# Modulation chunks in float32 and in three bfloat16 parts on four column groups, with another start-up order

## The chip, the cores and the metric

One core of a Trainium2 chip runs the kernel. Its engines are TensorE (PE, with its weight loads as PEld), VectorE (DVE), ScalarE (ACT), GpSimd (POOL) and SyncE (SP, which here only issues DMAs). The metric is device microseconds for one launch, lower is better.

## The reference, cut to what matters

Two blocks in sequence. The first has two layers over 256 tokens `x` and 256 context tokens `ctx`, width 1024; the second has two hybrid layers over `x` alone. The part that the change touches is the modulation of the first block: two condition vectors, `c` and `c_ctx`, go through one wide matrix per layer, and the twelve results scale, shift and gate the streams.

```python
def adaln(cond, w_ada, b_ada):
    m = jax.nn.silu(cond) @ w_ada + b_ada          # w_ada: 1024 x 6144 for each layer
    return jnp.split(m, 6, axis=-1)
...
    for l in range(DEPTH):                          # DEPTH = 2
        h = rms_norm(x, g_mix[l]) * (1 + sc1) + sh1
        hc = rms_norm(ctx, g_mix[l]) * (1 + csc1) + csh1
        ... h @ w_in, attention, Fourier mix ...
        x = x + gt1 * (o @ w_out[l])
        x = x + gt2 * swiglu(rms_norm(x, g_ffn[l]) * (1 + sc2) + sh2, w_gate[l], w_up[l], w_down[l])
        # the same for ctx in layer 0 only
```

Everything is float32.

## The kernel before, in words

**Weights.** All weights come as raw float32 tiles of 128x2048 (1 MB) on SP's queue, through three buffers (`raw`). For each 128x1024 piece ScalarE makes a rounded copy `whi` (L210) and VectorE the remainder `wlo` (L211), five buffers each. Products are three passes (`mm3`, L330 to L332): high by high, and the two cross terms.

**The modulation.** The 1024x6144 matrix of a layer is cut into 12 chunks of 512 columns, two raw tiles each; `(l, c)` is chunk c of layer l. `ada_chunk` (L463) splits four pieces into `whi` and `wlo` and runs 16 matmuls, with the four columns of `s4` (high and low part of both condition vectors) as the stationary operand and 512 weight columns moving (L480, L481). ScalarE copies the 4x512 result (L483), four small transposes put it on the partitions (L485), and three VectorE operations (L491 to L494) add the parts and the bias into `mod`. Chunk (1, 11) alone is `whole`: eight float32 matmuls on the raw tile (L475), no split.

**Where the chunks lie.** Chunks 2, 0, 3, 1 of layer 0 come before the first projection: chunk 2 ahead of the norms (L757), the others from `ada_start`. Two lie in the middle of layer 0's attention (`ada_mid`), four around its output projection (`ada_att`), six in its feed-forward steps (`ada_ffn`, keyed by the step f//2 of eleven). Layer 1's attention has two in `ada_mid` and four in `ada_att`, and two stand behind its second norm (`ada_gap`, L822).

**Start-up.** SP issues the identity, the conditions, `vec`, chunk 2's two raw tiles, then the context and the residual (`cs`, `xs`, 1 MB each, L760). Squares are made by ScalarE (L763) and summed over the eight k-tiles by one VectorE reduction per stream (L764); `sum_cols` (L351) sums over partitions by matmuls against a column of ones, and a chain of small VectorE operations and a transpose (`rsqrt`, `spread` L363) gives the row scale. Then two halves of the contraction follow in turn: gain, the weights' half, `modulate` of both streams (L520 to L522), 48 matmuls into four banks.

**Order.** The order on each engine is fixed when the program is built, by a scheduler that takes ready instructions by priority, in program order unless a function is `ranked` or stands in `together`, which moves a run of matmuls far ahead and lets it start after the operations it names. In the feed-forward network each step takes four pieces of gate and up weights and 96 matmuls of 512 columns; after steps 3, 7 and 10 the down projection of the group follows in `dn` banks. The attention sums `pv` (L625) already put two heads on two groups of 64 columns of the array, one behind the other.

Of the kernel before, what the change touches and what calls it, by code (L numbers as in the profile page):

```python
# [18 lines left out]
P = 128  # L19
KT = 8  # L20
# [195 lines left out]
        self.off = off  # L216


class WRows(Weights):


# [34 lines left out]
class Build:  # L256
# [17 lines left out]
    ada_whole = ((1, 11),)  # L274

    rank = {"weights": 100, "weigh": -200, "qk": -200, "rope": -300, "hd2": -300, "together": 3000}

    def __init__(self, ctx, tc, d, out):
        self.tc, self.nc, self.d, self.out = tc, tc.nc, d, out
# [180 lines left out]
            h0 += n  # L460


    def ada_chunk(self, l, c):  # L463

        nc = self.nc
        ps = self.bank("mm")
        off = (l * 12 + c) * P * 4096
        whole = (l, c) in self.ada_whole
        n = 2 if whole else 4
        if whole:  # L470
            for i in range(2):
                raw = self.wp.tile([P, RAW], F32, tag="raw", name="raw", bufs=self.raw_bufs)
                nc.sync.dma_start(raw, self.d["w_ada"][off + i * P * RAW:off + (i + 1) * P * RAW].rearrange("(p f) -> p f", p=P))
                for k in range(4):
                    nc.tensor.matmul(ps[:2, :], self.sil[:, 4 * i + k, :], raw[:, 512 * k:512 * k + 512], start=i + k == 0, stop=i == 1 and k == 3)  # L475
        else:
            ch = WRows(self, self.d["w_ada"], off, 512)
            for k in range(KT):
                hi, lo = ch.get(k)
                nc.tensor.matmul(ps[:4, :], self.s4[:, k, :], hi, start=k == 0, stop=False)  # L480
                nc.tensor.matmul(ps[:4, :], self.s4[:, k, :], lo, start=False, stop=k == KT - 1)  # L481
        rows = self.b1.tile([4, 512], F32, tag="rows", name="rows", bufs=1)
        nc.scalar.copy(rows[:n], ps[:n, :])  # L483
# [4 lines left out]
        src = ps[:, :8].rearrange("p (a b) -> p a b", b=2)  # L488
        if not whole:
            m = self.sp.tile([P, 4, 2, 2], F32, tag="adac", name="adac", bufs=2)  # L490
            nc.vector.tensor_copy(m.rearrange("p a b c -> p (a b c)"), ps[:, :16])  # L491
            nc.vector.tensor_tensor(dst, m[:, :, :, 0], m[:, :, :, 1], op=ALU.add)
            src = dst
        nc.vector.tensor_tensor(dst, src, b[:, :, None].to_broadcast([P, 4, 2]), op=ALU.add)  # L494

    def gain(self, l, which, ks=range(KT)):

# [6 lines left out]
    def norm_row(self, s):  # L504

        rb = self.acc[:, s * 256:s * 256 + 256]
        v = self.mean_eps(self.sum_cols(rb, 2), 2, D, "ms")
        self.nc.scalar.copy(rb, self.spread(self.rsqrt(v, 2, "rn"), 2))
        return rb

# [121 lines left out]
    def mixer1(self, l, h, o, first):  # L632
# [27 lines left out]
        for kind in range(2):  # L660
            ch = WRows(self, d["w_in"], base + (1 + kind) * P * 4096, 512)
            q0, f0 = (128, 0) if kind else (0, 384)
            for s in range(2 if full else 1):
                raws = [self.evac_raw(self.proj_t(ch, h, (2 * s + i,))[0], 512) for i in range(2)]
                if not kind:
                    r = self.head_rms(raws, 6, 0)
                for i in range(2):
                    q = raws[i][:, q0:q0 + 384]
                    if not kind:
                        self.scale_heads(q, r[:, 6 * i:6 * i + 6], 6)  # L670
                    if s == 0:
                        c, sn = (self.rc[:, i], self.rs[:, i]) if kind else (self.tqc[:, i], self.tqs[:, i])
                        q = self.rope(q, c, sn, 6, "rq")
                    elif not kind:
                        self.gain_heads(q, self.gq, 6)
                    dst = self.ap.tile([P, 6, P], F32R, tag="qt", name="qt", bufs=5)
                    self.to_qt(q, 6, dst)
                    self.qt[kind, 2 * s + i] = dst
                self.fourier(raws, f0, o[3 + kind], s * 256)
            for a in self.ada_mid[l] if kind else ():  # L680
                self.ada_chunk(*a)
            for s in range(2 if full else 1):
                self.heads1(kind, s, o)

# [36 lines left out]
    def block1(self, ctx):  # L721
# [7 lines left out]
        sil = self.sil = self.b1.tile([P, KT, 2], F32, name="sil")  # L729
        nc.scalar.activation(sil, ct, AF.Silu)  # L730
        self.s4 = self.b1.tile([P, KT, 4], F32R, name="s4")
        v = self.s4.rearrange("p k (s a) -> p k s a", a=2)
        nc.vector.tensor_copy(v[:, :, :, 0], sil)
        nc.vector.tensor_tensor(v[:, :, :, 1], sil, v[:, :, :, 0].bitcast(F32), op=ALU.subtract)
# [3 lines left out]
        nc.gpsimd.dma_start(wm, d["wm"])  # L738
# [12 lines left out]
        self.phase(self.att_banks)  # L751
        norm = ExitStack()
        self.np = norm.enter_context(tc.tile_pool(name="norm0", bufs=1, reuse_waits="tile"))
        nc.sync.dma_start(self.vec, d["vec"])
        nc.gpsimd.tensor_tensor(self.g12, self.vec[:, 128:136], self.vec[:, 136:144], op=ALU.mult)
        self.nt_bufs = 8
        self.ada_chunk(0, 2)  # L757
        rbs = [None, None]
        for s in (1, 0):
            nc.sync.dma_start(self.xs[s].rearrange("p a b -> p (a b)"), d["xT"][:, s * 2048:(s + 1) * 2048])  # L760
        for s in (1, 0):
            sq = self.np.tile([P, KT, 256], F32, tag="sq0", name="sq0", bufs=2)
            nc.scalar.activation(sq, self.xs[s], AF.Square)  # L763
            nc.vector.reduce_sum(self.acc[:, s * 256:s * 256 + 256], sq.rearrange("p k t -> p t k"), axis=AX.X)  # L764
            rbs[s] = self.norm_row(s)
        for l in range(2):

            both = (0, 1) if l == 0 else (0,)
# [3 lines left out]
            if l == 0:  # L772

                ps = [self.bank(tag) for tag in self.half_tags]
                for i in range(2):
                    ks = range(4 * i, 4 * i + 4)
                    for a in self.ada_start[i]:
                        self.ada_chunk(0, a)
# [9 lines left out]
                nc.sync.dma_start(c1, d["c1"])  # L788
                self.load_norms(l)
# [12 lines left out]
            for a in self.ada_att[l]:  # L802
                if isinstance(a, int):
                    self.out_first(l, a, o)
                else:
                    self.ada_chunk(*a)
            self.phase(self.lin_banks)
            norm = ExitStack()
            self.np = norm.enter_context(tc.tile_pool(name=f"norm{l + 1}", bufs=1, reuse_waits="tile"))
            with tc.tile_pool(name=f"ffn{l}", bufs=1, reuse_waits="tile") as fp:  # L810
                h = self.parts(fp, "F")
                for st in apart:
# [9 lines left out]
                    for a in self.ada_gap[l]:  # L822
                        self.ada_chunk(*a)
                f0 = 0
                dn = l * FT * P * 1024
                for gi, g in enumerate(FF_GROUPS):
                    acts = []
                    for f in range(f0, f0 + g, 2):
                        for a in self.ada_ffn[l].get(f // 2, ()):
                            self.ada_chunk(*a)  # L830
# [413 lines left out]
```

## Time and profile before

| | us |
|---|---|
| median of three runs (1584.55 to 1586.06) | 1584.88 |
| the profiled execution | 1584.88 |
| its span on the core | 1583.1 |
| PE busy in the span | 1535.0 |
| DVE busy | 1111.7 |
| ACT busy | 885.8 |

The span is the time from the first to the last instruction that the profile shows; the rest of the execution lies around it. A busy PE is not PE at its peak, since matmuls overlap and their records include the time to drain: two 512-column matmuls that each last 0.39 us can start 0.23 us apart. So PE work is counted from start to start.

### The profile page before, as it was taken

To read this page: it belongs to the slowest core of one execution; us is meant where nothing else is said; L and a number is where in the kernel's file an instruction comes from. 1 tells how busy PE (TensorE), PEld (TensorE's weight loads), DVE (VectorE), ACT (ScalarE), POOL (GpSimd) and SP (SyncE) were. 2 spreads that over 40 slices of the span, in tenths; PEclk is the share of its full clock that TensorE was granted. 3 is DMA by queue.
4 is the path that set the end of the run, shared out by engine and by line. 5 is a ranking of instruction groups with operands and counts; after the bars stand their busy time and mean duration, and the time that the engine had idled before them with its cause. 6 is when DMAs were issued, how large, how long until landed. Compare 5 with 4: busy or idle time off the path is not lost.

```text
span 1583.1 us, 25393 instructions
## 1 busy us (share of the span) xinstructions
PE 1535.0 (97%) x9826; PEld 1307.4 (83%) x9826; DVE 1111.7 (70%) x2332; ACT 885.8 (56%) x1590; POOL 71.0 (4%) x83
## 2 busy tenths in 40 slices
PE   4999999999999999999999999999999999999997
PEld 1776679878788778965779999998999999899997
DVE  7876988453433445989885555998867779987775
ACT  5567875342322234569764444667764456776542
POOL 0310000000000000010000000102000000201000
PEclk8999999999999999999999999999999999999998
DMA  7512443342332424444575554534344544334451
GB/s 285 199 54 81 173 160 136 132 164 104 133 107 81 149 98 162 154 156 156 201 261 181 184 179 161 170 139 152 115 160 160 184 142 155 133 117 170 146 178 51
DMA packets 36984, 238.38 MB, mean 151 GB/s; under 512 B 4224, under 2 KB 5888, under 8 KB 15104
## 3 DMA queue, kind: packets, MB, share of 16 engines
q1 hardware_dynamic: 36576, 236.14, 42.8%
q8 instruction: 77, 1.26, 0.3%
q0 software_dynamic: 288, 0.62, 0.3%
q14 instruction: 43, 0.35, 0.1%
HBM read 236.32 MB, written 1.05 MB: 150 GB/s over the span
## 4 chain that ended last, share of the span: by engine, by line
PE 83%; DVE 10%; ACT 3%; issue 2%; DMA 1%; SPq 0%; POOL 0%; DVEq 0%; ACTq 0%; POOLq 0%
PE mm L331 10%; PE mm L332 10%; PE mm L330 10%; PE g L332 6%; PE g L331 6%; PE g L330 6%; PE dn L331 5%; PE dn L330 5%; PE dn L332 5%; DVE wlo L211 3%; PE mm L481 2%; PE mm L480 2%; PE pv L625 2%; PE tr L617 2%; PE pv L959 1%
## 5 line engine op out<-in xcount | busy, mean ns | idle before, releaser
L210 ACT CAST whi<-raw 128x1024 fp32r<-128x1024 f32 (+4 forms) x484 | 462.7, 967 | 500.3 <-PE mm L331 137.7
L211 DVE TENSOR_TENSOR wlo<-raw,whi 128x1024 fp32r<-128x1024 f32 (+4 forms) x484 | 541.9, 1129 | 183.7 <-ACT whi L210 180.7
L331 PE MATMUL dn<-Hl,whi 128*128 128x256 f32 (+1 forms) x520 | 161.2, 310 | 0.0
L332 PE MATMUL dn<-Hh,wlo 128*128 128x256 f32 (+1 forms) x520 | 160.6, 309 | 0.0
L330 PE MATMUL dn<-Hh,whi 128*128 128x256 f32 (+1 forms) x520 | 160.5, 309 | 0.0
L332 PE MATMUL mm<-Hh,wlo 128*128 128x256 f32 (+1 forms) x512 | 149.8, 293 | 0.0
L331 PE MATMUL mm<-Hl,whi 128*128 128x256 f32 (+1 forms) x512 | 149.1, 291 | 0.0
L330 PE MATMUL mm<-Hh,whi 128*128 128x256 f32 (+1 forms) x512 | 149.0, 291 | 0.0
L330 PE MATMUL mm<-whi,Hh 128*128 128x384 f32 (+2 forms) x352 | 128.8, 366 | 0.0
L332 PE MATMUL mm<-whi,Hl 128*128 128x384 f32 (+2 forms) x352 | 127.6, 363 | 0.0
L331 PE MATMUL mm<-wlo,Hh 128*128 128x384 f32 (+2 forms) x352 | 127.1, 361 | 0.0
L332 PE MATMUL g<-Fh,wlo 128*128 128x256 f32 (+1 forms) x368 | 122.0, 332 | 0.5 <-DVE wlo L211 0.5
L330 PE MATMUL mm<-Fh,whi 128*128 128x256 f32 (+1 forms) x368 | 122.1, 332 | 0.3 <-ACT Fh L521 0.3
L332 PE MATMUL mm<-Fh,wlo 128*128 128x256 f32 (+1 forms) x368 | 122.1, 332 | 0.0
L331 PE MATMUL mm<-Fl,whi 128*128 128x256 f32 (+1 forms) x368 | 122.0, 332 | 0.0
L331 PE MATMUL g<-Fl,whi 128*128 128x256 f32 (+1 forms) x368 | 121.7, 331 | 0.0
L330 PE MATMUL g<-Fh,whi 128*128 128x256 f32 (+1 forms) x368 | 121.7, 331 | 0.0
L331 PEld LDWEIGHTS dn<-Hl,whi 128*128 128x128 f32 x520 | 99.1, 191 | 5.8 <-DVE Hl L848 0.6
L330 PEld LDWEIGHTS dn<-Hh,whi 128*128 128x128 f32 x520 | 99.0, 191 | 5.6 <-issue 0.4
L332 PEld LDWEIGHTS dn<-Hh,wlo 128*128 128x128 f32 x520 | 99.1, 191 | 5.0
L331 PEld LDWEIGHTS mm<-Hl,whi 128*128 128x128 f32 x512 | 97.7, 191 | 1.1 <-issue 0.3
L330 PEld LDWEIGHTS mm<-Hh,whi 128*128 128x128 f32 x512 | 97.8, 191 | 0.7
(282 smaller groups left out, 3361.3 us busy)
## 6 DMA issues: line engine op xcount, KB each, us to landing
raw<-in_w_ada_dram SPq DMA_DIRECT2D x48, 1024.0 KB, 4.9
raw<-in_w_gu_dram SPq DMA_DIRECT2D x44, 1024.0 KB, 4.8
raw<-in_w_mix_dram SPq DMA_DIRECT2D x32, 1024.0 KB, 4.8
raw<-in_w_in_dram SPq DMA_DIRECT2D x40, 768.0 KB, 4.3
raw<-in_w_in_dram SPq DMA_DIRECT2D x20, 1024.0 KB, 4.9
raw<-in_w_dn_dram SPq DMA_DIRECT2D x16, 1024.0 KB, 4.9
raw<-in_w_dn_dram SPq DMA_DIRECT2D x12, 768.0 KB, 4.3
raw<-in_w_out_dram SPq DMA_DIRECT2D x8, 1024.0 KB, 4.8
```

What stands on the lines that cost most here:

```text
L210: nc.scalar.copy(hi[:, :m], x)
L211: nc.vector.tensor_tensor(lo[:, :m], x, hi[:, :m].bitcast(F32), op=ALU.subtract)
L330: nc.tensor.matmul(out, lhs[0], rhs[0], start=start, stop=False)
L331: nc.tensor.matmul(out, lhs[0], rhs[1], start=False, stop=False)
L332: nc.tensor.matmul(out, lhs[1], rhs[0], start=False, stop=stop)
L480: nc.tensor.matmul(ps[:4, :], self.s4[:, k, :], hi, start=k == 0, stop=False)
L481: nc.tensor.matmul(ps[:4, :], self.s4[:, k, :], lo, start=False, stop=k == KT - 1)
L617: nc.tensor.transpose(ps[:, (2 * j + qt) * P:(2 * j + qt + 1) * P], p[i][:, qt, c:c + P], self.ident)
L625: first(nc.tensor.matmul(pv[i * 64:i * 64 + 64, :256], v, pts[i][0][:, j * 256:j * 256 + 256], start=b == 0 and j == 0, stop=b == nk // 2 ...
L959: f(nc.tensor.matmul(pv[64 * i:64 * i + 64, c], vs[i][j], pt[:, d], start=first and j == 0, stop=last and j == 1))
```

## The change

`ada_chunk` gets a `way`. **whole**: for each of the two raw tiles, four float32 matmuls straight from the tile, the four k-tiles on the four groups of 32 output partitions (`ps[32 * g:32 * g + 32]`), with `s32`, the two conditions padded with zeros to 32 columns, as the stationary operand. **thirds**: the raw tile's float32 numbers are read as bfloat16 halves; the upper halves are used in place (`upper`, every second 16-bit number), two VectorE subtractions per 1024 columns make the middle and the low part, and 12 bfloat16 matmuls per tile run on the same four groups, with `s6`, three bfloat16 parts of both conditions. `ada_end` copies 128x512 instead of 4x512, makes four 128x128 transposes, and sums the groups and parts by two small reductions. The ten chunks (0, 0) to (0, 9) go whole; the other 14 go in thirds in layer 0's feed-forward steps 1 to 10, and layer 1 keeps none. `cs` and `xs` are loaded ahead of `vec` and of chunk 2; their squares are made in halves and summed by 16 matmuls per stream against the ones, in place of the reduction; the context's norm stands ahead of chunk 2. Chunk 0 comes in the first half of the first projection, 3 and 1 in the second. The mask `wm` (a cast DMA on POOL's queue) moves behind the first projection.

```diff
-    ada_start = ((0, 3, 1), ())
-    ada_mid = ((0, 4), (0, 5)), ((1, 4), (1, 5))
-    ada_att = ((0, 6), 0, (0, 7), (0, 9), 1, (0, 8)), ((1, 6), (1, 7), 0, 1, (1, 9), (1, 8))
-    ada_gap = (), ((1, 10), (1, 11))
-    ada_ffn = {3: ((0, 11), (0, 10)), 4: ((1, 0),), 8: ((1, 1),), 10: ((1, 3), (1, 2))}, {}
+    ada_start = ((0,), (3, 1))
+    ada_mid = ((0, 4), (0, 5)), ()
+    ada_att = ((0, 6), 0, (0, 7), (0, 9), 1, (0, 8)), (0, 1)
+    ada_ffn = {1: ((0, 10),), 2: ((0, 11),), 3: ((1, 0),), 4: ((1, 1),), 5: ((1, 2),), 6: ((1, 3),), 7: ((1, 4), (1, 5)),
+               8: ((1, 6), (1, 7)), 9: ((1, 8), (1, 9)), 10: ((1, 10), (1, 11))}, {}
...
+        for i in range(2):
+            raw = self.wp.tile([P, RAW], F32, tag="raw", name="raw", bufs=self.raw_bufs)
+            nc.sync.dma_start(raw, ...)
+            if way == "whole":
+                for g in range(4):
+                    nc.tensor.matmul(ps[32 * g:32 * g + 32, :], self.s32[:, 4 * i + g, :], raw[:, 512 * g:512 * g + 512],
+                                     start=i == 0, stop=i == 1)
+                continue
+            mid, low, made = [], [], []
+            for a in range(2):
+                x = raw[:, 1024 * a:1024 * a + 1024]
+                r = self.wp.tile([P, 1024], F32, tag="wlo", name="wmid", bufs=self.w_bufs)
+                lo = self.wp.tile([P, 1024], BF16, tag="whi", name="wlow", bufs=self.w_bufs)
+                nc.vector.tensor_tensor(r, x, upper(x), op=ALU.subtract)
+                made.append(nc.vector.tensor_tensor(lo, r, upper(r), op=ALU.subtract))
...
+            with self.together(made) as add:
+                for n, part in enumerate(parts):
+                    for g in (3, 2, 1, 0):
+                        add(nc.tensor.matmul(ps[32 * g:32 * g + 32, :], self.s6[:, 4 * i + g, :], part(g),
+                                             start=i + n == 0, stop=i == 1 and n == 2))
+        self.ada_end(l, c, ps, way)
...
+        nc.scalar.copy(rows, ps)
         for j in range(4):
-            nc.tensor.transpose(ps[:, j * n:j * n + n], rows[:n, j * P:(j + 1) * P], self.ident[:n, :n])
+            nc.tensor.transpose(ps[:, j * P:(j + 1) * P], rows[:, j * P:(j + 1) * P], self.ident)
...
+        for s in range(2):
+            nc.vector.tensor_reduce(dst[:, :, s], v[:, :, :, n * s:n * s + n], axis=AX.XY, op=ALU.add)
...
-            nc.vector.reduce_sum(self.acc[:, s * 256:s * 256 + 256], sq.rearrange("p k t -> p t k"), axis=AX.X)
-            rbs[s] = self.norm_row(s)
+            ps = self.bank("tr")
+            for j in range(2):
+                for k in range(KT):
+                    nc.tensor.matmul(ps[:, j:j + 1], sq[:, k, j * P:(j + 1) * P], self.ones, start=k == 0, stop=k == KT - 1)
+            rbs[s] = self.norm_row(s, ps[:, :2])
```

## Rows read from the trace of the kernel before

**Rows 1.** Page, busy time, share of the span and instructions of each engine.
```profile
PE 1535.0 (97%) x9826; PEld 1307.4 (83%) x9826; DVE 1111.7 (70%) x2332; ACT 885.8 (56%) x1590; POOL 71.0 (4%) x83
```
**Rows 2.** Windows of the start; columns: stretch, length, each engine's busy time, clock, DMA.
```profile
core 0: us, PE busy (x) PEld busy (x) DVE busy (x) ACT busy (x) POOL busy (x), PEclk, DMA share, GB/s
0.00:45.00 45.00, 23.66 (x90) 8.54 (x90) 33.39 (x66) 28.43 (x34) 1.12 (x6) 0.89 0.79 293
45.00:67.00 22.00, 21.75 (x98) 17.72 (x98) 20.51 (x43) 13.84 (x28) 9.23 (x16) 1.00 0.67 241
...
14.00:17.00 3.00, 2.51 (x9) 0.63 (x6) 2.00 (x2) 1.88 (x2) 0.00 (x0) 1.00 1.03 431
...
20.00:25.00 5.00, 0.70 (x3) 0.17 (x2) 4.68 (x11) 2.81 (x3) 0.00 (x0) 0.50 0.44 184
```
**Rows 3.** Timeline of the start: start, duration, instruction, idle time before it.
```profile
13.52 1.91 ACT L763 ACTIVATE sq<-cs 128x2048 f32<-128x2048 f32 x1 [0.50 <-DMA cs<-in_xT_dram]
15.46 3.72 DVE L764 TENSOR_REDUCE acc<-sq 128x256 f32<-128x2048 f32 x1 [1.00 <-ACT sq L763]
...
44.54 0.63 PE L330 MATMUL sc<-whi,Hh 128*128 128x512 f32 x2
...
67.13 0.39 PE L332 MATMUL pv<-whi,Hl 128*128 128x512 f32 x1
```
**Rows 4.** Timeline behind layer 1's output projection: a chunk's split matmuls.
```profile
797.47 0.40 PE L480 MATMUL mm<-whi,s 128*4 128x512 f32 x1
797.70 0.39 PE L481 MATMUL mm<-wlo,s 128*4 128x512 f32 x1
```
**Rows 5.** Timeline, twelve records of the whole chunk (1, 11), two per matmul.
```profile
804.35 5.31 PE L475 MATMUL mm<-raw,sil 128*2 128x512 f32 x12
```
**Rows 6.** Timeline, attention sums on two column groups (two records per matmul) and transposes.
```profile
118.86 1.08 PE L625 MATMUL pv<-pt,v 128*64 128x256 f32 x8
119.87 0.65 PE L617 MATMUL tr<-ident,p 128*128 128x128 f32 x4
...
132.17 1.95 PE L625 MATMUL pv<-pt,v 128*64 128x256 f32 x16
```
**Rows 7.** Timeline, the small matmuls of a chunk's end and of the column sums.
```profile
19.24 1.01 PE L351 MATMUL tr<-ones,acc 128*128 128x1 f32 x4 [1.66 <-DVE acc L764]
...
802.70 0.41 PE L485 MATMUL mm<-ident,rows 4*128 4x4 f32 x4
```
**Rows 8.** Layer 0's attention: the window's row, and the split matmuls in it.
```profile
100.00:230.00 130.00, 128.27 (x745) 84.43 (x744) 107.48 (x313) 104.49 (x238) 6.00 (x14) 1.00 0.33 114
...
L480 PE MATMUL mm<-whi,s 128*4 128x512 f32 x48 | 19.4, 404 | 0.0
```
**Rows 9.** Groups by line, 240 to 640 us: count, busy us, mean ns, idle before.
```profile
L211 DVE TENSOR_TENSOR wlo<-raw,whi 128x1024 fp32r<-128x1024 f32 (+2 forms) x103 | 119.0, 1167 | 77.0 <-ACT whi L210 74.7
...
L845 DVE TENSOR_TENSOR fa<-fa,g 128x512 f32<-128x512 f32 x22 | 15.2, 689 | 73.2 <-PE g L332 72.5 <-ACT fa L844 0.7
L848 DVE TENSOR_TENSOR Hl<-fa,Hh 128x512 fp32r<-128x512 f32 x22 | 15.1, 684 | 0.0
```
**Rows 10.** Layer 1's attention: the window's row, and the split matmuls in it.
```profile
680.00:780.00 100.00, 97.03 (x560) 63.13 (x558) 89.74 (x215) 81.12 (x158) 7.33 (x7) 1.00 0.46 154
...
L480 PE MATMUL mm<-whi,s 128*4 128x512 f32 x44 | 17.7, 401 | 0.0
```
**Rows 11.** Timeline and window: layer 1's feed-forward start, and the kernel's last norm.
```profile
809.59 0.38 PE L330 MATMUL mm<-Fh,whi 128*128 128x256 f32 x1
...
1571.02 0.42 DVE L1201 SCALAR_TENSOR_TENSOR xs<-g,xs 128x256 f32<-128x256 f32 x1 [1.46 <-PE g L332]
...
1575.58 0.66 PE L363 MATMUL tr<-ident,rf 128*128 128x128 f32 x2 [2.51 <-DVE rf L344]
...
1575.00:1580.00 5.00, 0.66 (x2) 0.29 (x2) 3.58 (x11) 0.00 (x0) 0.00 (x0) 0.52 0.40 129
```

More of the change, by code (lines that the diff above doesn't have):

```diff
@@ L216, in __init__, with upper @@
         self.off = off
+def upper(x):
+    x = x.bitcast(BF16)
+    if len(x.shape) == 3:
+        return x.rearrange("p a (n two) -> p a n two", two=2)[:, :, :, 1]
+    return x.rearrange("p (n two) -> p n two", two=2)[:, :, 1]
 class WRows(Weights):
@@ L267 @@
     first_tags = ("mm", "mm", "sc", "sc")
[L269 to L276 removed]
+    ada_start = ((0,), (3, 1))
[3 more added lines that the diff above has]
+               8: ((1, 6), (1, 7)), 9: ((1, 8), (1, 9)), 10: ((1, 10), (1, 11))}, {}
+    rank = {"weights": 100, "weigh": -200, "qk": -200, "rope": -300, "hd2": -300, "rows": -60, "together": 3000}
     def __init__(self, ctx, tc, d, out):
@@ L460, in to_kt, with ada_chunk @@
             h0 += n
-    def ada_chunk(self, l, c):
+    def ada_chunk(self, l, c, way, tag="mm"):
         nc = self.nc
-        ps = self.bank("mm")
+        ps = self.bank(tag)
         off = (l * 12 + c) * P * 4096
[L468 to L483, printed above, removed]
@@ new lines, in ada_chunk @@
+        for i in range(2):
+            raw = self.wp.tile([P, RAW], F32, tag="raw", name="raw", bufs=self.raw_bufs)
+            nc.sync.dma_start(raw, self.d["w_ada"][off + i * P * RAW:off + (i + 1) * P * RAW].rearrange("(p f) -> p f", p=P))
+            if way == "whole":
[10 more added lines that the diff above has]
+                made.append(nc.vector.tensor_tensor(lo, r, upper(r), op=ALU.subtract))
+                mid.append(upper(r))
+                low.append(lo)
+            h = upper(raw)
+            parts = [lambda g, t=t: t[g // 2][:, g % 2 * 512:g % 2 * 512 + 512] for t in (low, mid)]
+            parts.append(lambda g: h[:, 512 * g:512 * g + 512])
+            with self.together(made) as add:
[3 more added lines that the diff above has]
+                                             start=i + n == 0, stop=i == 1 and n == 2))
@@ L484, in ada_chunk, with ada_end @@
+        self.ada_end(l, c, ps, way)
+    @ranked("rows")
+    def ada_end(self, l, c, ps, way):
+        nc = self.nc
+        rows = self.b1.tile([P, 512], F32, tag="rows", name="rows", bufs=1)
+        nc.scalar.copy(rows, ps)
         for j in range(4):
-            nc.tensor.transpose(ps[:, j * n:j * n + n], rows[:n, j * P:(j + 1) * P], self.ident[:n, :n])
+            nc.tensor.transpose(ps[:, j * P:(j + 1) * P], rows[:, j * P:(j + 1) * P], self.ident)
         dst = self.mod[l][:, c * 4:c * 4 + 4, :]
@@ L487, in ada_chunk @@
         b = self.vec[:, l * 64 + c * 4:l * 64 + c * 4 + 4]
[L488 to L494, printed above, removed]
+        v = ps.rearrange("p (j g a) -> p j g a", j=4, g=4)
@@ L496, in gain @@
+        n = 1 if way == "whole" else 3
+        for s in range(2):
+            nc.vector.tensor_reduce(dst[:, :, s], v[:, :, :, n * s:n * s + n], axis=AX.XY, op=ALU.add)
+        nc.vector.tensor_tensor(dst, dst, b[:, :, None].to_broadcast([P, 4, 2]), op=ALU.add)
     def gain(self, l, which, ks=range(KT)):
@@ L502, in gain, with norm_row @@
                                             g[:, :, None].to_broadcast([P, n, 2]), op0=ALU.add, op1=ALU.mult)
-    def norm_row(self, s):
+    def norm_row(self, s, sums=None):
         rb = self.acc[:, s * 256:s * 256 + 256]
-        v = self.mean_eps(self.sum_cols(rb, 2), 2, D, "ms")
+        v = self.mean_eps(self.sum_cols(rb, 2) if sums is None else sums, 2, D, "ms")
         self.nc.scalar.copy(rb, self.spread(self.rsqrt(v, 2, "rn"), 2))
@@ L680, in mixer1 @@
             for a in self.ada_mid[l] if kind else ():
-                self.ada_chunk(*a)
+                self.ada_chunk(*a, "whole")
             for s in range(2 if full else 1):
@@ L753, in block1 @@
         self.np = norm.enter_context(tc.tile_pool(name="norm0", bufs=1, reuse_waits="tile"))
+        for s in (1, 0):
+            nc.sync.dma_start(self.xs[s].rearrange("p a b -> p (a b)"), d["xT"][:, s * 2048:(s + 1) * 2048])
         nc.sync.dma_start(self.vec, d["vec"])
@@ L756, in block1 @@
         self.nt_bufs = 8
-        self.ada_chunk(0, 2)
         rbs = [None, None]
         for s in (1, 0):
-            nc.sync.dma_start(self.xs[s].rearrange("p a b -> p (a b)"), d["xT"][:, s * 2048:(s + 1) * 2048])
-        for s in (1, 0):
             sq = self.np.tile([P, KT, 256], F32, tag="sq0", name="sq0", bufs=2)
-            nc.scalar.activation(sq, self.xs[s], AF.Square)
-            nc.vector.reduce_sum(self.acc[:, s * 256:s * 256 + 256], sq.rearrange("p k t -> p t k"), axis=AX.X)
-            rbs[s] = self.norm_row(s)
+            for i in range(2):
+                nc.scalar.activation(sq[:, 4 * i:4 * i + 4], self.xs[s][:, 4 * i:4 * i + 4], AF.Square)
+            ps = self.bank("tr")
[3 more added lines that the diff above has]
+            rbs[s] = self.norm_row(s, ps[:, :2])
+            if s:
+                self.ada_chunk(0, 2, "whole")
         for l in range(2):
@@ L777, in block1 @@
                     for a in self.ada_start[i]:
-                        self.ada_chunk(0, a)
+                        self.ada_chunk(0, a, "whole")
                     self.gain(0, 0, ks)
@@ L805, in block1 @@
                 else:
-                    self.ada_chunk(*a)
+                    self.ada_chunk(*a, "whole")
             self.phase(self.lin_banks)
```

23 lines of the change are left out of this document (14 added, 9 removed).

## The prediction

> **What bounds the kernel now.** I read the busy shares first: PE 1535.0 of 1583.1 us, VectorE 70%, ScalarE 56% [rows 1]. So time is won where PE has less to do, and where PE is not dense although it is called busy. The windows come next. In the first 45 us PE is busy for 23.7 us and VectorE for 33.4, and between 20 and 25 us VectorE has 4.68 of 5 us while the DMA falls to 184 GB/s, against 431 in 14 to 17 us [rows 2]: the raw tiles are not given back, so the loads wait for VectorE's splits and for its 3.72 us reductions [rows 3]. The first projection starts at 44.54 and its last matmul at 67.13 [rows 3]. After that PE is bound nearly everywhere, and a chunk costs there what its matmuls take from start to start.
>
> **Cost of a chunk.** Split matmuls start 0.23 us apart [rows 4], so before a chunk is 16 x 0.23 = 3.7 us, and its four small transposes add (0.41 - 0.20)/3 = 0.07 each, some 0.3 [rows 7]: 4.0 us.
> Whole: one group's two records of 512 float32 columns take 5.31/12, about 0.43 each [rows 5], so eight matmuls in a row would be 6.9 us. Four column groups at once are not in this trace, but two are: the 16 records of `pv` last 1.95 us with one 0.38 us tail, about 0.107 per 256-column record [rows 6], half of 0.43/2 = 0.215. So two groups run fully side by side. I take four as four: per tile 2 x 0.43 = 0.86, plus 0.2 for going into and out of this form of use (the eight records last 1.08, with 4 x 0.215 for the pairs and the tail [rows 6], which leaves it between nothing and 0.2). Two tiles are 2.1 us. The four 128x128 transposes are the L617 kind, (0.65 - 0.27)/3 = 0.13 each, 0.45 [rows 6]. Together 2.55 us; bounds 2.2 and 7.5 (no overlap).
> Thirds: 12 matmuls of 512 columns per tile; four at once is 3 x 0.23 = 0.7, but 12 weight-load and matmul pairs at 0.07 [rows 7] need 0.84, and I take that, with 0.2: 2.1 for two tiles and 2.55 with the transposes; bounds 2.0 and 6.4.
> The Trainium skill ("TensorE: Matmul & The Clock Gate", Packing small matmuls) states 2.38x for three column groups of 32. Kept at that share four would give 3.2x, an estimate from that page: a whole chunk 3.0 us, thirds about as here, and the sum below 3 us more. No run here shows three or four groups yet.
> The 128x512 copy by ScalarE has as many columns as the 4x512 one and costs the same; two small reductions and an addition replace three small VectorE operations, between -0.1 and +0.5 us per chunk, off PE's path, taken as nothing.
>
> **Start-up: -16 us.** The load order is now cs, xs, then eight chunk tiles and two weight tiles: 12 x 1.05 MB. A whole chunk's tile is free as soon as its four matmuls are done, about 1 us after landing, and the queue is three deep, so I let the loads run at 0.40 MB/us from 2.6 us: 34 us, with 2 us for hiccups 36. VectorE loses 16 remainders of 1.2 us and two reductions, 27 us of its 33. The sums of squares cost PE 32 records per stream at 0.25 us (the row at the lower clock [rows 7]), 8 us each, while PE would wait for loads anyway; if that cover failed it would be 5 us. The first half of the projection needs chunks 2 and 0 only and can run from about 26 to 37 us; the second half starts at about 39, behind the last weights' split and chunk 1's shift, and takes 11 us. It ends at 51 in place of 67. Bounds -8 (loads stalled as in 20 to 25 us for part of the way) and -20. The mask's DMA passes POOL's table work in the queue by its one issue, under 1 us, and is read far later; cost nothing.
>
> **Layer 0's attention: -9.** Six chunks at 4.0 become six at 2.55 on a PE that is busy 128.3 of 130 us [rows 8]. The 48 casts and remainders that go (ScalarE and VectorE are at 104 and 107 of 130) can thin out PE's short waits. Bounds -14 and +21 (6 x 3.5).
>
> **Layer 0's feed-forward: +15.** Before, six chunks, 24 us; after, 14 x 2.55 = 36, so +12. VectorE: eight subtractions per chunk at the 1.17 us of L211 [rows 9], 9.4, plus 0.5. A step's own VectorE work is 4 x 1.17 + 2 x (0.69 + 0.68) = 7.4 us [rows 9], its PE work 96 x 0.23 = 22. A step with one chunk has 17 us on VectorE beside 24.5 on PE; a step with two (7 to 10) has 27 beside 27. So the last four steps are even, and I add 3 us of waits. These subtractions have a 16-bit operand read at every second number, which no row shows; bounds 0.6 and 2.3 us, value that of L211. What waits behind them on VectorE is the step's own remainders and the multiply that frees the gate banks; both have a projection or two of slack. Bounds of the term +4 and +66.
>
> **Layer 1: -25.** In 680 to 780 us 44 of L480 run and about as many of its partner L481 [rows 10], 20 us, with five chunk ends 22 us. PE is not dense there: ScalarE and VectorE have 81 and 90 of 100, of which the chunks' casts and remainders are some 22 and 25. So all three engines get lighter by a quarter, and I let the stage give back 20 us; up to 780 to 797, 2 more. Behind the output projection, chunks (1, 10) and (1, 11) fill PE from 797.47 to 809.59 [rows 4, 11]. The chain of that norm, without them, is like the last norm's, 1571.02 to 1576.24 [rows 11], with half a microsecond ahead and a copy, a multiply and the first shift behind it, 7.4 us in all: -4.7. But now PE idles, and the granted clock falls from 2.4 to 1.2 GHz as at 1575 to 1580 (0.52) [rows 11]: +2, as matmuls at half rate after the gap. Sum -25; bounds -5 and -37.
>
> **Sum.** -16 - 9 + 15 - 25 = -35 on a span of 1583.1: 1548. The profiled execution took 1584.88, 1.8 more than its span and exactly the median of the runs shown. Forecast 1550.
>
> **Rivals.**
> A. Groups overlap only two at a time: 1575. For it: two are all that a row shows. Against: pairs overlap without loss [rows 6]. Whole 4.3, thirds 3.6: attention +2, feed-forward +27, start -14, layer 1 -25, together -10.
> B. No overlap on 32 columns: 1640 (attention +21, feed-forward +66, start -6, layer 1 -25). Against: `pv`.
> C. The other side: VectorE becomes the bound in the feed-forward steps. With 2.34 us per subtraction, twice L211, a two-chunk step has 46 us on VectorE beside 27, four of them 75, less 27 that the down projection after step 7 absorbs, and one-chunk steps add 13: some 57 more than forecast, 1607. It decides from about 2.1 us per subtraction, where the gain of 35 is eaten. For it: VectorE takes 134 us more work there. Against: L211 also reads two operands and is no slower for it.
> The Trainium skill ("VectorE: DVE Perf Modes", What auto-detection actually checks) lets a two-operand operation go at double rate only if all its tensors are 16-bit and contiguous; these are mixed, so by it they go at the single rate of L211, neither 0.6 nor 2.3. By that rule C is a small case.
> D. Layer 1's attention is bound by its own chain of scores, exponentials, copies and transposes, and the chunks only filled its holes: layer 1 gives 5, not 25: 1570. For it: PE is called busy there with records that overlap. Against: ScalarE and VectorE also lose a quarter.
>
> **How the numbers follow.** Forecast 0.58 (own range 1532 to 1566), A 0.14, D 0.12, C 0.08, B 0.05, else 0.03. The range takes in A, D and the good ends of start and layer 1 (-62 together with +4 to +8 in the feed-forward): 1521 to 1588, leaving out B, most of C and a little below. Within 0.2% (about what a measurement tells from no change, 1581.7 to 1588.1) lie the joint bad ends of A and D, 0.05; slower 0.12; faster 0.83.
>
> **What would show it.** Right: first projection's last matmul near 51 us and a DMA of over 350 GB/s up to 35 us; records of a whole chunk starting in fours, 0.43 us per four; subtractions near 1.17 us; PE without long waits in the steps 7 to 10; layer 1's attention some 20 us shorter, and a hole of 7 us at a clock near 0.5 ahead of its feed-forward. Wrong: starts of the groups in pairs (A) or singly (B); PE waiting for `wlow` (C); the same 100 us in layer 1's attention with PE idle (D).

## The result, and the profile after

The changed kernel takes 1600.41 us (median of 4 runs, 1597.59 to 1604.64) against 1584.72 us beside it: ratio 1.0099, 95% interval [1.0079, 1.0119]. It is slower by 1%; the forecast was 1550 and the range ended at 1588. The profiled execution took 1597.64 us, its span is 1595.9 us (before 1583.1), so the traces account for 12.8 of the 15.7 us between the medians; the two executions above 1603 us, at a mean granted clock of 0.983 in place of 0.987, have no trace.

PE has less to do, and the time is longer all the same. The page's busy line of after, beside [rows 1]:

```profile
PE 1523.2 (95%) x9994; PEld 1306.8 (82%) x9994; DVE 1129.7 (71%) x2357; ACT 800.5 (50%) x1500; POOL 66.6 (4%) x83
```

To see where, I cut both traces at the same events: layer 0's first and last attention exponential, the first feed-forward matmul, layer 1's first normed tile, its first and last exponential, its first feed-forward matmul. Columns as in [rows 2]. First layer 0's attention, the way from its last exponential to the feed-forward, the feed-forward, layer 1's attention and the way from there to its feed-forward, in the kernel before:

```profile
105.60:222.20 116.60, 116.04 (x673) 75.76 (x672) 96.53 (x286) 95.77 (x220) 1.39 (x1) 1.00 0.34 115
222.20:255.60 33.40, 32.38 (x258) 29.70 (x256) 29.07 (x71) 21.40 (x41) 3.58 (x12) 1.00 0.53 185
255.60:618.40 362.80, 362.18 (x1679) 287.32 (x1678) 160.69 (x225) 120.57 (x153) 0.00 (x0) 1.00 0.36 124
708.20:769.40 61.20, 59.26 (x371) 38.03 (x370) 55.20 (x145) 54.48 (x115) 1.55 (x2) 1.00 0.46 153
769.40:809.60 40.20, 39.82 (x243) 24.49 (x242) 34.37 (x74) 26.84 (x45) 0.00 (x0) 1.00 0.70 242
```

The same five stretches after:

```profile
116.20:222.40 106.20, 102.81 (x618) 63.61 (x616) 67.57 (x247) 71.51 (x190) 1.56 (x2) 1.00 0.24 87
222.40:265.20 42.80, 42.53 (x314) 37.12 (x314) 33.98 (x85) 24.75 (x48) 4.21 (x12) 1.00 0.68 243
265.20:646.20 381.00, 373.73 (x1950) 288.29 (x1949) 262.38 (x338) 102.03 (x137) 0.00 (x0) 0.99 0.46 162
734.50:790.00 55.50, 49.72 (x311) 35.40 (x309) 39.94 (x119) 41.75 (x99) 1.93 (x2) 0.97 0.19 56
790.00:822.00 32.00, 21.56 (x154) 18.20 (x154) 18.73 (x43) 14.27 (x27) 0.00 (x0) 0.87 0.38 133
```

| stage | forecast | measured |
|---|---|---|
| start-up (to the first exponential, 105.6 and 116.2) | -16 | +10.6 |
| layer 0's attention and output projection | -9 | -1.0 (-10.4, then +9.4) |
| layer 0's feed-forward | +15 | +18.2 |
| layer 1 up to its feed-forward | -25 | -15.4 (projections -1.5, attention -5.7, behind it -8.2) |
| the rest | 0 | +0.4 |

**The start.** The first projection runs from 40.12 to 78.13 us, where before had 44.54 to 67.13. Windows of after: PE works for most of 18 to 24 us, while the DMA moves nothing; a second hole stands at 48 to 54 us.

```profile
12.00:18.00 6.00, 3.94 (x19) 3.85 (x19) 1.68 (x11) 0.39 (x1) 0.00 (x0) 1.00 0.87 365
18.00:24.00 6.00, 5.13 (x23) 4.77 (x24) 0.27 (x2) 0.37 (x1) 0.00 (x0) 1.00 0.00 0
48.00:54.00 6.00, 6.00 (x28) 4.70 (x26) 0.17 (x1) 0.00 (x0) 3.96 (x16) 1.00 0.13 49
60.00:66.00 6.00, 2.45 (x14) 0.87 (x14) 3.64 (x10) 3.37 (x6) 0.00 (x0) 1.00 1.00 422
```

PE's timeline of after shows why: the two sums of squares (L798) stand ahead of chunk 2's first matmuls (L482), and the first half of the projection ahead of the matmuls at 54.00. In both places the three raw tiles had landed and could not be given back; behind the second hole the next load is issued at 55.12.

```profile
8.95 6.98 PE L798 MATMUL tr<-ones,sq 128*128 128x1 f32 x32 [8.95 <-ACT sq L794]
18.40 0.66 PE L370 MATMUL tr<-ident,rn 128*128 128x128 f32 x2 [2.47 <-issue]
19.53 6.98 PE L798 MATMUL tr<-ones,sq 128*128 128x1 f32 x32 [0.46 <-ACT acc L532]
26.44 1.93 PE L482 MATMUL mm<-raw,s 128*32 128x512 f32 x8
...
54.00 2.78 PE L482 MATMUL mm<-raw,s 128*32 128x512 f32 x24
...
55.12 0.33 SPq L479 DMA_DIRECT2D raw<-in_w_ada_dram  x1
```

**Layer 0's output projection.** What the attention gained, it lost to the stretch behind it: 314 matmul records there, before 258. SP's queue shows part of the cause. Before, and then after (start, time that the issues took, how many): w_out's first loads came at 160.64 and 188.55, after at 175.50 and 218.10, behind chunk loads that waited.

```profile
64.50 89.23 SPq L203 DMA_DIRECT2D raw<-in_w_ada_dram  x6
160.64 0.33 SPq L203 DMA_DIRECT2D raw<-in_w_out_dram  x1
162.99 19.71 SPq L203 DMA_DIRECT2D raw<-in_w_ada_dram  x4
188.55 0.33 SPq L203 DMA_DIRECT2D raw<-in_w_out_dram  x1
```

```profile
75.46 96.24 SPq L479 DMA_DIRECT2D raw<-in_w_ada_dram  x6
175.50 0.33 SPq L203 DMA_DIRECT2D raw<-in_w_out_dram  x1
183.20 32.40 SPq L479 DMA_DIRECT2D raw<-in_w_ada_dram  x4
218.10 0.33 SPq L203 DMA_DIRECT2D raw<-in_w_out_dram  x1
```

The waits of after give the queue's releaser (total us, times, longest): PE's whole-chunk matmuls held a load back for 64.2 us at once. The queue stood before too, but for VectorE's remainders: 153.0 us between 60 and 260 us, 40.0 the longest.

```profile
SPq L479 <- PE mm L482: 128.2, 12, 64.2
```

**The feed-forward.** PE's waits in this stage, by the waits view of after (before there is one, of 0.3 us):

```profile
PE dn L500 <- DVE wlow L491: 4.5, 3, 1.9
PE mm L337 <- ACT Fh L545: 1.4, 1, 1.4
PE mm L337 <- ACT whi L210: 1.0, 1, 1.0
PE g L339 <- DVE wlo L211: 0.3, 1, 0.3
```

Half of that stands in one place, step 8, the second step with two chunks and the first behind a down projection; 1.9 us of the waits for `wlow` stand in step 1, and steps 7, 9 and 10, with two chunks as well, have none. Window and timeline of step 8:

```profile
560.35:571.30 10.95, 7.30 (x39) 4.18 (x38) 9.91 (x14) 4.58 (x5) 0.00 (x0) 0.69 0.72 258
```

```profile
511.51 42.90 SPq L479 DMA_DIRECT2D raw<-in_w_ada_dram  x4
...
558.74 5.22 SPq L203 DMA_DIRECT2D raw<-in_w_gu_dram  x2
...
561.46 2.35 DVE L491 TENSOR_TENSOR wlow<-wmid 128x1024 bf16<-128x1024 f32 x2
562.73 0.40 PE L500 MATMUL dn<-wlow,s 128*32 128x512 bf16 x4 [1.78 <-DVE wlow L491]
...
563.53 1.99 ACT L210 CAST whi<-raw 128x1024 fp32r<-128x1024 f32 x2 [4.20 <-DMA raw<-in_w_gu_dram]
...
564.63 0.80 PE L337 MATMUL mm<-Fh,whi 128*128 128x512 f32 x1 [1.04 <-ACT whi L210]
...
566.25 0.62 PE L500 MATMUL dn<-wlow,s 128*32 128x512 bf16 x4 [0.83 <-DVE wlow L491]
```

The chunks' loads keep the queue from 511.51 to 554.41, so the step's own weights are asked for at 558.74 only; PE waits for a subtraction, for the weights, for a subtraction again, 3.65 us in all, and at the lower clock the eight matmuls from 567.65 to 571.2 then start some 0.43 us apart in place of 0.23: 1.6 us more.

### The profile page after: what moved, and what is told of

Same layout as the page of the kernel before. It is cut to its first block, busy times and chain, and to the rows that moved or that the text cites. A ratio compares the mean times of both kernels' runs of the same rounds, so it can differ in the third digit from the quotient of the medians.

```text
span 1595.9 us, 25544 instructions
## 1 busy us (share of the span) xinstructions
PE 1523.2 (95%) x9994; PEld 1306.8 (82%) x9994; DVE 1129.7 (71%) x2357; ACT 800.5 (50%) x1500; POOL 66.6 (4%) x83
## 4 chain that ended last, share of the span: by engine, by line
PE 82%; DVE 10%; ACT 4%; issue 2%; DMA 1%; POOL 0%; DVEq 0%; SPq 0%; ACTq 0%; POOLq 0%
PE mm L338 10%; PE mm L337 10%; PE mm L339 10%; PE g L337 6%; PE g L338 6%; PE g L339 6%; PE dn L338 4%; PE dn L337 4%; PE dn L339 4%; DVE wlo L211 3%; PE pv L649 2%; PE tr L641 2%; PE mm L482 1%; PE dn L500 1%; PE pv L994 1%
## 5 line engine op out<-in xcount | busy, mean ns | idle before, releaser
L210 ACT CAST whi<-raw 128x1024 fp32r<-128x1024 f32 (+4 forms) x392 | 368.6, 948 | 400.9 <-PE mm L338 82.6
L211 DVE TENSOR_TENSOR wlo<-raw,whi 128x1024 fp32r<-128x1024 f32 (+4 forms) x392 | 430.4, 1105 | 129.3 <-ACT whi L210 128.0
```

What stands on the lines that cost most here:

```text
L210: nc.scalar.copy(hi[:, :m], x)
L211: nc.vector.tensor_tensor(lo[:, :m], x, hi[:, :m].bitcast(F32), op=ALU.subtract)
```

## The experiments

Beside every one the kernel before ran at 1584.6 to 1585.2 us; ratios are to it. Four traces with the changed start as it is (after, `ffn_whole`, `l1_back`, `l1_back_whole`) have the first exponential at 116.2 to 118.1 us, so a difference of 2 us at the start says nothing.

**The start.** Four kernels, each the changed one with one thing of its start undone, the last with all three.

`chunk2_first`:
```diff
         rbs = [None, None]
+        self.ada_chunk(0, 2, "whole")
...
-            if s:
-                self.ada_chunk(0, 2, "whole")
```


> The changed kernel with one line moved: chunk 2 of layer 0 stands ahead of both norms in the program, not between them; all else as in the changed kernel, whose loads stood still from 18 to 26 us and from 48 to 54 us and whose first attention exponential was at 116.2 us (before: 105.6). Theory H (the three raw tiles are held because PE reaches the chunk's matmuls late in its fixed order, and the loads wait for the tiles): chunk 2's matmuls run as its tiles land, near 16 us, the first hole closes, the first projection starts some 8 us earlier (near 32), the second hole stays; 7 us faster than the changed kernel. Rival S (the 14 us of column sums on PE at its lower clock are themselves what the start waits for): the sums are all still there, so 2 us or less.

1602.52 us, 1.0112 [1.0097, 1.0127]; first exponential 118.8. A miss: chunk 2's matmuls stayed at 26.6, behind the sums, so the order written in the program isn't PE's order there, and both holes stayed.

`sums_dve`:
```diff
...
-                for k in range(KT):
-                    nc.tensor.matmul(ps[:, j:j + 1], sq[:, k, j * P:(j + 1) * P], self.ones, ...)
-            rbs[s] = self.norm_row(s, ps[:, :2])
+            nc.scalar.activation(sq, self.xs[s], AF.Square)
+            nc.vector.reduce_sum(self.acc[:, s * 256:s * 256 + 256], sq.rearrange("p k t -> p t k"), axis=AX.X)
+            rbs[s] = self.norm_row(s)
```


> The changed kernel with the squares summed by VectorE again (one square of 128x2048 and one reduction per stream) instead of 32 matmuls on PE; chunk 2 stays between the two norms. Theory H: PE is free for chunk 2 as soon as the context's norm is through, near 19 us, so most of the first hole closes, 6 us faster than the changed kernel, and the second hole stays. Rival S: all of the sums' 14 us comes back, 12 us or more. If chunk2_first gains as much as this one, it is the place of the chunk and not the sums' length.

1595.57 us, 1.0070 [1.0053, 1.0087]; first exponential 112.1, first chunk matmul 14.8 in place of 26.4. From 18 to 24 us the DMA still moves nothing, from 24 to 30 it moves 341 GB/s in place of 19: the sums on PE make about half of the first hole.

`start_at_once`:
```diff
-    ada_start = ((0,), (3, 1))
+    ada_start = ((0, 3, 1), ())
```


> The changed kernel with chunks 0, 3 and 1 all ahead of the first half of the first projection, as before the change; sums on PE and chunk 2's place as in the changed kernel. Theory H: the second hole (48 to 54 us, tiles of chunks 3 and 1 held behind the first half's 48 matmuls) closes, the first half starts later, some 8 us, and the second follows without a wait: the projection ends some 6 us earlier than at 77, 6 us faster than the changed kernel. Rival S: nothing is taken from PE's sums, so no gain, and the later first half may cost up to 5 us.

1597.55 us, 1.0078 [1.0063, 1.0093]; first exponential 114.3. The second hole goes (320 GB/s from 48 to 54 us), the first stays. The gain of 2.9 us is not clear of the spread (the two intervals overlap), and less than the 6 expected.

`start_both` (all three edits):

> The changed kernel with all three: chunk 2 ahead of the norms, squares summed by VectorE, chunks 0, 3, 1 ahead of the first half. The load order (context and residual first) and the four column groups stay. Theory H: no raw tile is held behind other PE work, the loads run at over 350 GB/s to about 38 us, the first projection ends near 54 us in place of 77: 22 us faster than the changed kernel, 1576. Rival L (the new load order itself costs, since context and residual come ahead of the weights): the projection ends no earlier than before the change, 67 us, and the gain is 10 us or less.

1591.23 us, 1.0041 [1.0026, 1.0056]; first exponential 107.1. So 9.1 of the 10.6 us are these edits. The -16 does not come back even so: the loads of w_in wait for raw tiles (first one issued at 35.4), and the projection starts at 44.7, as before. `pack_only` below, with the load order of before, has its first exponential at 107.5, so the new load order neither gives nor costs.

**Where the chunks stand.** `l1_back` takes eight of layer 1's chunks out of the feed-forward and puts them back, whole, where before had them; `l1_back_whole` makes the six that are left whole too, `ffn_whole` leaves all fourteen there and makes them whole.
```diff
-    ada_mid = ((0, 4), (0, 5)), ()
-    ada_att = ((0, 6), 0, (0, 7), (0, 9), 1, (0, 8)), (0, 1)
-    ada_ffn = {1: ((0, 10),), 2: ((0, 11),), ...
+    ada_mid = ((0, 4), (0, 5)), ((1, 4), (1, 5))
+    ada_att = ((0, 6), 0, (0, 7), (0, 9), 1, (0, 8)), ((1, 6), (1, 7), 0, 1, (1, 9), (1, 8))
+    ada_ffn = {2: ((0, 10),), 3: ((0, 11),), 4: ((1, 0),), 6: ((1, 1),), 8: ((1, 3),), 9: ((1, 2),)}, {}
...
+                    for a in ((), ((1, 10), (1, 11)))[l]:
+                        self.ada_chunk(*a, "whole")
```


> The changed kernel with eight chunks of layer 1 taken out of layer 0's feed-forward and put back to where the kernel before has them (layer 1's projections, attention and the gap behind its output projection), whole on four column groups; six thirds chunks stay in layer 0's feed-forward. Theory 'layer 1's attention is bound by its own chain and chunks only fill holes of PE there': the feed-forward gives 8 x 2.55 = 20 us and some 4 of waits in its two-chunk steps, layer 1 takes back at most 10: 1586. Rival 'a chunk costs PE the same wherever it stands' (as the forecast had it): 20 out, 20 in, only the waits of the two-chunk steps go: 1597. Rival 'the chunks hold up the chain in layer 1 as before': layer 1 takes back all its 15 us, 1592.

1587.80 us, 1.0016 [1.0007, 1.0025]. The feed-forward gives 28 us (353.0 in place of 381.0), layer 1 takes 13 (160.3 in place of 147.3). Windows of `l1_back`, layer 1's attention and the way to its feed-forward:

```profile
708.70:768.40 59.70, 58.99 (x373) 34.95 (x372) 38.62 (x126) 41.73 (x101) 1.94 (x2) 1.00 0.50 174
768.40:809.10 40.70, 34.50 (x253) 23.19 (x252) 23.38 (x67) 18.09 (x37) 0.00 (x0) 0.96 0.71 262
```

With the chunks PE is busy for 9.3 us more in the attention than after, and the stretch is only 4.2 longer: they fill holes.

> As l1_back, and the six chunks that stay in layer 0's feed-forward whole too, so that no subtraction is left anywhere. Theory 'waits for the subtractions are a cost of their own': 3 us less than l1_back. Rival 'only steps with two chunks wait for VectorE': same as l1_back within 1 us.

1586.67 us, 1.0011 [1.0001, 1.0021]: the intervals of the two overlap, and the feed-forward takes 353.3 and 353.0 us, so the subtractions of one chunk per step cost 1 us at most.

```diff
-                            self.ada_chunk(*a, "thirds", "dn")
+                            self.ada_chunk(*a, "whole", "dn")
```


> The changed kernel with all fourteen feed-forward chunks whole in place of thirds: 112 subtractions on VectorE go, PE's matmul time per chunk stays about the same (8 float32 matmuls at 0.43 per four against 24 at 0.23 per four). Theory 'PE waits for VectorE's subtractions': layer 0's feed-forward gets 5 to 7 us shorter (the waits of dn matmuls for wlow, and the ones they push on), 1594. Rival 'a chunk costs PE its matmuls and its ends, waits are small': within 2 us of the changed kernel, 1599 to 1601. Rival 'the subtractions make the whole +18 by slowing the step's own remainders': 12 us or more less, 1588.

1620.93 us, 1.0225 [1.0210, 1.0240]. All three theories missed: no subtraction is left, and it is 20 us slower, 399.3 us in the feed-forward. Waits and SP's queue of `ffn_whole` in that stage:

```profile
PE dn L482 <- DMA raw<-in_w_ada_dram: 10.7, 4, 2.7
...
518.70 48.34 SPq L479 DMA_DIRECT2D raw<-in_w_ada_dram  x4
```

PE now waits for the chunk's own load. That made me form the theory of the raw ring: a chunk is loaded into the ring of three raw tiles, which the split of the kernel before gave back early, and a whole chunk keeps two of them until PE comes to its matmuls. What is behind it in the one queue, the second chunk and the weights, can't be asked for. Thirds keep the tile as well, for their last four matmuls (`dn<-raw`), but those stand in `together`, which a whole chunk's do not: the queue waited for such matmuls 132 us in this stage, 25.6 the longest, and 113 and 9.8 in after. Way and place in PE's order change at once in this run, and no run separates them.

**Packing alone, and the ring.** `pack_only` is the kernel before with every chunk whole on four groups, in its old place.

> The kernel before with nothing changed but the way of each chunk: all 24 whole on four column groups (and the chunk's end as in the changed kernel); load order, sums of squares by VectorE, first projection in one go and every chunk's place as before. Theory 'a packed chunk saves PE 1.4 us only where PE is dense, in the feed-forward (six chunks) and the gap (two), and next to nothing in the two attention stages and the start, which are bound by their own chains': 1584.6 - 8 x 1.4 - 2 = 1571. Rival, the forecast's 'a chunk costs PE its matmuls everywhere': 20 chunks x 1.4 behind the start = 28 less and some 3 at the start, 1553. Rival 'float32 loads in whole tiles hold up the other loads': no faster than 1582.

1588.19 us, 1.0022 [1.0012, 1.0032]: PE has 16 us less work (1519.0 us busy), and nothing is won, as the last rival had it. In step 10 of the feed-forward two chunks follow one another. PE's timeline of `pack_only`:

```profile
593.12 0.66 PE L510 MATMUL dn<-ident,rows 128*128 128x128 f32 x4
596.42 1.80 PE L481 MATMUL dn<-raw,s 128*32 128x512 f32 x8 [2.65 <-DMA raw<-in_w_ada_dram]
598.96 1.11 PE L510 MATMUL dn<-ident,rows 128*128 128x128 f32 x4 [0.74 <-ACT rows L508]
599.99 0.80 PE L336 MATMUL mm<-Fh,whi 128*128 128x512 f32 x1
```

`land_pack` is `pack_only` with the chunk loaded elsewhere, in two rings of the split that whole chunks leave idle:
```diff
-            raw = self.wp.tile([P, RAW], F32, tag="raw", name="raw", bufs=self.raw_bufs)
-            nc.sync.dma_start(raw, ...)
...
+                land = [self.wp.tile([P, 1024], F32, tag=t, name="land", bufs=self.w_bufs) for t in ("whi", "wlo")]
+                for a in range(2):
+                    nc.sync.dma_start(land[a], src[:, 1024 * a:1024 * a + 1024])
...
-                    nc.tensor.matmul(..., raw[:, 512 * g:512 * g + 512],
+                    nc.tensor.matmul(..., land[g // 2][:, g % 2 * 512:g % 2 * 512 + 512],
```


> The kernel of run pack_only (the kernel before, every chunk whole on four column groups, 1588 us) with one thing changed: a whole chunk's tile isn't loaded into the ring of three raw tiles but into one tile each of the rings of the split's two results (128x1024, five each), which a whole chunk leaves unused; so loads are twice as many and half as large. Theory 'a whole chunk holds raw tiles until PE gets to its matmuls, so the loads behind it in the in-order queue stand, and weights come late': in layer 0's attention the waits of the queue for PE (64.2 us the longest) go, the first loads of w_out are issued near 160 us again in place of 167 to 175, the output projection behind the last exponential shrinks from 43 to 33 us, the chunk pairs of the feed-forward no longer wait for DMA; together 10 + 8 and some 4 elsewhere: 1566. Rival 'the attention stages are bound by their own chain and the chunks fill holes': only the feed-forward's and the gap's waits go, 1577. Rival 'the raw ring has nothing to do with it': within 2 us of 1588.

1570.72 us, 0.9911 [0.9897, 0.9926]: 17.5 us come back from where a load lands, with the same matmuls on the same numbers. The ring's theory holds; its sizes were off: the feed-forward gave 14.2 (351.9 in place of 366.1), layer 0's attention with its output projection 4.5, layer 1's attention 4.1, and the start lost 3.9. The loads are half as large here too, which this run does not separate; the next one keeps their size. And `l1_back_whole`, with the raw ring but one whole chunk to a step, has 353.3 us in the feed-forward: what costs there is two whole chunks in a row on three raw tiles.

`raw4w4` keeps the landing of `pack_only`, with four raw tiles and four of each of the split's:
```diff
-    raw_bufs, w_bufs, ... = 3, 5, ...
+    raw_bufs, w_bufs, ... = 4, 4, ...
```


> The kernel of run pack_only with four raw tiles in place of three, and four of each of the split's results in place of five (the same memory). Theory of the raw ring: one more load ahead takes away about half of what land_pack takes away, 1577. Rival 'four split buffers cost as much in the dense stages': 1588 or more. Rival 'the ring has nothing to do with it': 1588.

1578.85 us, 0.9960 [0.9945, 0.9975]: one tile more brings half (9.3 us), as expected.

`land_after` is the changed kernel with the same landing for its whole chunks:

> The changed kernel with the same landing of whole chunks in the split's rings; the feed-forward's thirds keep the raw ring. Theory of the raw ring: the start's two holes in the DMA (18 to 26, 48 to 54 us) close at least in part and layer 0's attention with its output projection gets 8 us shorter: first exponential 108 in place of 116, first matmul of the feed-forward 249 in place of 265: 1584. Rival 'program order and the norm chain make the start late': first exponential stays at 114 to 116, 1592. Rival 'no effect of the ring': 1600.

1598.65 us, 1.0091 [1.0075, 1.0108]: a miss by its total, and not clear of the changed kernel's spread. Attention and output projection take 146.0 us in place of 149.0, but the first exponential comes at 117.7, and the feed-forward, whose thirds keep the raw ring, takes 383.0. The first hole of the start goes (419 GB/s from 18 to 24 us), and the projection starts no earlier (43.52): the next chunks' loads are issued from 29.84 to 53.34 only, into the split's rings, which the projection's own weights use too. So this run moves the wait at the start to other rings, and does not show what the raw ring alone costs there.

**A version that beats both.** `land_mid` is `land_pack` with the start's four chunks in the raw ring; `land_spread` also has one chunk to a step in the feed-forward.
```diff
-            if way == "whole":
+            if way == "whole" and (l or c > 3):
```


> The kernel of run land_pack, but the four chunks of the start go through the ring of raw tiles again (as in pack_only); all later whole chunks land in the split's rings. Theory 'at the start the split's rings are needed for the first projection's own weights, so landing there delays it (first exponential 111.4 in land_pack, 107.5 in pack_only)': 107.5 again, and 3.9 us less than land_pack in all, 1567. Rival 'what the start gives is eaten by the attention's chain': 1571.

1565.50 us, 0.9884 [0.9868, 0.9901]; first exponential 108.1. Windows of `land_mid`, the first three stretches of above:

```profile
108.10:216.30 108.20, 106.16 (x641) 67.12 (x639) 70.29 (x255) 74.06 (x193) 1.59 (x2) 1.00 0.34 117
216.30:254.40 38.10, 38.07 (x294) 33.86 (x291) 32.54 (x79) 23.75 (x44) 2.99 (x12) 1.00 0.49 169
254.40:606.40 352.00, 351.35 (x1679) 281.49 (x1678) 132.82 (x201) 97.30 (x129) 0.00 (x0) 1.00 0.38 128
```

> The kernel of run land_mid, and the six feed-forward chunks one to a step (steps 2, 3, 4, 6, 8, 9) in place of two in steps 3 and 10. Theory 'two whole chunks in a step cost through the loads they hold up': what is left of it in land_pack (other matmuls 340.6 us against 338.6 before in that stage) goes, 2 us less than land_mid. Rival 'with the landing the pairs cost nothing any more': same as land_mid within 1 us.

1569.25 us, 0.9902 [0.9887, 0.9916]. The feed-forward is the same (352.7 us): pairs of chunks cost nothing once their loads stand elsewhere. Of the 4 us between the two, 3.2 lie on the way from layer 1's attention to its feed-forward (48.3 and 45.1 us), where the granted clock is 0.89 in place of 0.96; why it is lower was not tried.

## Why the prediction was wrong

**Cost of a chunk: right.** In after the four groups' records start within 20 ns of each other (26.439, 26.446, 26.453, 26.459), and from 54.00 on every 0.43 us, the time of one record alone [rows 5]; rivals A and B fall. The Trainium skill ("TensorE: Matmul & The Clock Gate", Packing small matmuls) has 2.38x for three groups; four are 4x here, so the measurement decides against the share carried over. From start to start, chunks and transposes of the feed-forward take 28.1 us for fourteen, waits included, and the 71 records ahead of them 8.4 more than others: 2.6 each, for 2.55, or 2.3 without the 4.5 us of waits for `wlow`. The subtractions took 1.22 us each, for 1.17 assumed, the single rate that the Trainium skill ("VectorE: DVE Perf Modes", What auto-detection actually checks) expects of mixed operands:

```profile
L491 DVE TENSOR_TENSOR wlow<-wmid 128x1024 bf16<-128x1024 f32 x56 | 67.3, 1219 | 0.4
L490 DVE TENSOR_TENSOR wmid<-raw 128x1024 f32<-128x1024 f32 x56 | 66.9, 1219 | 17.4 <-PE mm L339 8.5 <-PE dn L500 7.9 <-DMA raw<-in_w_ada_dram 0.9
```

**Start-up, -16: failed.** The step that failed is "a whole chunk's tile is free as soon as its four matmuls are done, about 1 us after landing". The matmuls run when PE comes to them: 26.4 us for tiles that were there at 18, since the sums of squares, which the prediction put in PE's waiting time, stand ahead of them. Those 2 x 8 us (measured 2 x 7) were not hidden; they set the loads, and `sums_dve` gives 4.1 us back. The bound of 5 us for this was right in size but missed that the loads stand still meanwhile. Running the projection by halves made the same again (48 to 54 us). Behind the holes the projection's matmuls also run at a low clock, 0.70 from 42 to 48 and 0.72 from 66 to 72 us with PE busy for 6.00 and 5.63 of 6, some 3.5 us by an estimate from these windows. Why the start gains nothing with all three edits undone (`start_both`) beyond the raw tiles that w_in's loads wait for was not tried.

**Layer 0's attention, -9: failed in its place.** The stage itself gave 10.4 us, and the output projection took back 9.4. w_out's loads came 15 and 30 us later, of which the later start is 10.6. In `land_mid` its first loads are issued from 67.39 on, and the projection still takes 38.1 us, before 33.4: the late loads are about half of the 9.4, and the other half stays open. I counted casts and matmuls and not what the split had also done: to empty the raw tile early. With the ring freed (`land_mid`) attention and output projection take 146.3 us, 3.7 less than before, not 9; that PE's holes there are worth only part of a chunk is my reading, which no run tests alone.

**Feed-forward, +15: right by size, not by its parts.** Forecast 12 for more chunks and 3 for waits; the waits are 7.2 us and the slow matmuls behind them 1.6, which leaves 9.4 of the 18.2 for the chunks. "The last four steps are even" held in steps 7, 9 and 10 and failed in step 8, where the chunks' loads kept the step's own weights from being asked for. Rival C had the sign (PE waits for wlow), but the subtractions are only part of the cause: `ffn_whole`, without one, waits for loads and is slower, and with one chunk to a step (`l1_back`) the stage falls by 28 us for eight chunks, 3.5 each.

**Layer 1, -25: failed, by rival D's mechanism.** The stage gave 15.4, between the forecast's 25 and D's 5. Taking the chunks away took 9.5 us of PE's busy time out of the attention, and 5.7 us of the stage: PE, VectorE and ScalarE all sit idle there now (49.7, 39.9 and 41.8 of 55.5). "All three engines get lighter by a quarter" was no reason for the chain to be shorter. The way behind it gave 8.2; 4.7 less 2 was forecast for its last 12 us and up to 2 more for 780 to 797. The hole is there at the lower clock. Window of after:

```profile
816.00:822.00 6.00, 1.38 (x6) 0.92 (x6) 3.56 (x17) 0.91 (x3) 0.00 (x0) 0.58 0.38 158
```

The forecast missed by 47.8 us of span: 26.6 at the start, 8.0 in layer 0's attention, 3.2 in its feed-forward, 9.6 in layer 1 and 0.4 behind it. Of these only layer 1's had a rival (D, priced at 20); the start, the largest, had a bound of -8 and the 5 us of the sums, and no rival in which it gets later. One share is not separated by any run: the mean granted clock is 0.987 after and 0.994 before, which over the spans is up to 11 us of PE's full rate (an estimate), part of it in stretches where PE waits anyway.

## What to carry to other kernels

A split, a cast or a copy that moves data out of a landing buffer is also what gives the buffer back; before it is removed, ask until when the tile is then held and which loads stand behind it in the same in-order queue. When work is taken off an engine and the time stays, look for the load that is issued later than before. Work put "into the waiting time" of an engine is hidden only if nothing in that engine's order behind it gives back a buffer.

## What the runs showed that I had not expected

The matmul rate after waits is a price of its own: three waits of 3.65 us in all between 560.95 and 566.25, then eight matmuls at half rate (granted clock 0.69 from 560.35 to 571.3). And the clock's column does not show every slow stretch: at 26.4 us the whole chunk's fours start 0.85 us apart, twice the 0.43 of 54 us, while the window 26 to 28 us has a granted clock of 1.00. The first change of the clock that this trace holds, to full speed, stands at 35.3 us, and up to 35.0 the fours start 0.85 us apart: ahead of the first recorded change the column's 1.00 is no measurement.
